# Seven block products for each pair of the last four gate tiles, with the combined inputs formed in the places of q

## The chip, the cores and the metric

One core of a Trainium2 chip runs the whole layer as one program. The metric is the device time of one execution in microseconds (us), the median of several runs. Engines: PE multiplies matrices, DVE, ACT and POOL work on vectors, SP issues transfers; POOL and ACT can issue transfers too. Each engine works through its instructions in the order in which the built program has them, and waits on semaphores for what other engines and transfers deliver.

## The reference

A transformer layer on 1024 tokens of width 1024 with 256 context tokens. The part that matters here is the input projection of the modulated tokens and the gates:

```python
h = x * (1.0 + scale1) + shift1
proj = h @ w_in + b_in                      # q_a, k_a, v_a, q_b, k_b, v_b, then 2 x 1024 gate columns
o_a = _windowed_attention(q_a, k_a, v_a, k_a_c, v_a_c, sink)
o_b = _global_attention(q_b, concat(k_b, k_b_c), concat(v_b, v_b_c))
g_a, g_b = jnp.split(jax.nn.sigmoid(proj[..., OFF_GA:]), 2, axis=-1)
y = (g_a * (o_a @ w_branch_a) + g_b * (o_b @ w_branch_b)) @ w_out
x = _layer_norm(DEEPNORM_ALPHA * x + gate1 * y, ln1_g, ln1_b)
```

A gated convolutional feed-forward part with a second layer norm follows. All inputs and the output are 32-bit floats.

## The kernel before

Every product is made from three matmuls on pairs of a rounded value and its rest: `split` (L335) casts to the high half and subtracts for the low half, `mm3` (L344) adds high x high, high x low and low x high into one PSUM bank of 128x512. `wsplit` (L418) makes such a pair from a 128x512 block of weights: the high half on ACT, the low half on DVE, or on POOL for gate weights.

The stage of the projections holds the modulated x, transposed, as pairs `hT[k]` (hh, hl: 128 rows of the width by 1024 tokens, k from 0 to 7) for its whole length. It runs a list of steps, `order` (L943 on), from the numbers `GORD`: so many gates, then group qa, gates, group qb, gates, group ka (keys and values of tokens 0 to 639), gates, group kb (the other tokens and the context), gates. `GORD = 3, 4, 4, 1, 4` puts one gate between ka and kb and four behind kb. A group step multiplies one k with the group's four or five token tiles (12 or 15 matmuls) and holds a PSUM bank for each of them; a gate (128 of the 2048 gate columns) is two steps of 24 matmuls, one for each half of the tokens (`gate`, L908). It ends with the sigmoid on ACT and a transfer of the result to DRAM (`sgd`). Eight PSUM banks rotate among all of these.

Around the matmuls, a step loads the weights of the step five ahead (`wload1`, three buffers) and splits those of the step three ahead (`wpair`, four pairs of buffers), both in the order of the code. Up to the end of ka the orders of DVE and SP are the code's; behind that a scheduler sets them, and PE's order follows the code of the steps. Between the matmuls `side_step` (L932) takes the work of finished groups from a queue, one piece of each running item at a time. For a key and value tile that is `kv_post` (L628): s1 adds the bias on DVE out of PSUM (L633, tile `kv`, two buffers), turns the first keys (L532 to L540) and splits the values; s2 scales and turns the other keys and makes the pair `ks` (L341, L342); s3 transposes `ks` on PE into `ktr` (L664), four matmuls of 128x128, which ACT copies to the key tables KL and KC. Tiles `pw` (five buffers) hold the intermediate values and `ks`. Sets 0 to 4 are the tiles of ka, 5 to 9 those of kb. Two more sets, `qtr` (L699), transpose q for the first two units of attention.

Before that, q of both branches was written to SBUF tiles `Q[br, t]`, 128x2x512 each, in eight places of a pool (`hslot` names the place of each tile). Attention begins on PE right behind the last gate and reads KL, KC, V and Q in an order that a planner sets.

## Time and profile before

| | |
|---|---|
| median of 3 runs | 1532.02 us (1530.24 to 1532.84) |
| profiled execution | 1530.37 us, span of its instructions 1528.6 us, clock 0.998 |
| PE, DVE, ACT, POOL busy | 1512.9, 1144.8, 802.1, 773.5 us |
| group ka on PE | 220.15 to 247.35 us |
| gate between ka and kb | 247.35 to 258.24 us |
| group kb, with seven sets of transpositions | 258.24 to 288.06 us |
| four gates, with five sets | 288.06 to 333.48 us |

The page of the profile has for each engine its busy time, groups of instructions by line, and 40 slices of the span (the stretch above lies in slices 6 to 9). The views by window, by timeline and by group answer the same for a chosen stretch. A line of the timeline has the start, the duration, engine, line of the code, operation, output and inputs with buffer numbers left out, shape, how many in a row, and in brackets the idle time ahead of it with what ended that. In the groups the mean duration is in ns.

### The profile page before, as it was taken

Reading aid. Unit: us, or ns where it says so; the run is one execution under the profiler, and the core shown is the slowest. Engines: PE = TensorE matmul, PEld = TensorE weight load, DVE = VectorE, ACT = ScalarE, POOL = GpSimd, SP = SyncE. Lnnn points to the kernel's source line nnn. Section 1 sums busy time; section 2 is a strip of 40 time slices with the busy share of each in tenths; the row PEclk is TensorE's granted clock in tenths of the full one; section 3 lists DMA queues with packets and bytes.
Section 4 is the critical chain, followed back from the end, with each engine's and each line's share of the span. In section 5 each row is a group of like instructions: output and inputs, shape, how many; then the busy total and the mean of one; then the engine's idle time right before and its main releaser. Section 6 shows DMA issues by size and latency. Waiting matters only on the chain. (4 is left out here: it accounts for less than half of the span.)

```text
span 1528.6 us, 21924 instructions
## 1 busy us (share of the span) xinstructions
PE 1512.9 (99%) x7652; PEld 1269.9 (83%) x7652; DVE 1144.8 (75%) x1719; ACT 802.1 (52%) x1404; POOL 773.5 (51%) x737
## 2 busy tenths in 40 slices
PE   9999999999999999999999999999999999999997
PEld 7888888888988888888788988888888888888886
DVE  7488847627776777787665878888888887656797
ACT  5422223449887777798332574444444444435543
POOL 0365303418887565574333556666676674021063
PEclk9999999999999999999999999999999999999999
DMA  9667663312256663742460222333334446996723
GB/s 379 236 234 254 213 239 110 100 49 56 57 151 157 176 149 79 169 95 68 169 173 35 97 86 108 112 110 112 112 102 111 110 111 177 373 281 207 253 91 111
DMA packets 111873, 229.73 MB, mean 150 GB/s; under 512 B 13489, under 2 KB 27313, under 8 KB 111666
## 3 DMA queue, kind: packets, MB, share of 16 engines
q1 hardware_dynamic: 96464, 199.20, 39.0%
q0 software_dynamic: 10400, 20.19, 8.4%
q10 hardware_dynamic: 4898, 8.94, 1.6%
q8 instruction: 60, 0.98, 0.3%
q14 instruction: 51, 0.42, 0.1%
HBM read 177.09 MB, written 65.87 MB: 159 GB/s over the span
## 5 line engine op out<-in xcount | busy, mean ns | idle before, releaser
L1151 DVE TENSOR_TENSOR lo<-pt,hi 128x512 fp32r<-128x512 f32 x188 | 126.4, 688 | 42.8 <-ACT hi L1145 41.3
L342 DVE TENSOR_TENSOR ld<-rd,hd 128x1024 fp32r<-128x1024 f32 x77 | 97.8, 1287 | 49.6 <-ACT hd L337 47.4
L1145 ACT CAST hi<-pt 128x512 fp32r<-128x512 f32 x188 | 109.6, 584 | 47.3 <-PE pt L808 39.1
L337 ACT CAST hd<-rd 128x1024 fp32r<-128x1024 f32 x77 | 79.4, 1050 | 85.8 <-PE p L347 55.7
L345 PE MATMUL p<-hd 128*128 128x512 f32 x264 | 103.2, 391 | 0.0
L346 PE MATMUL p<-ld,hd 128*128 128x512 f32 x264 | 102.8, 389 | 0.2 <-DVE ld L342 0.2
L347 PE MATMUL p<-hd,ld 128*128 128x512 f32 x264 | 102.8, 389 | 0.0
L817 PE MATMUL av<-lo,VT 128*128 128x512 f32 x236 | 101.5, 435 | 0.2 <-POOL lo L1151 0.2
L817 PE MATMUL av<-hi,VT 128*128 128x512 f32 x236 | 100.5, 433 | 0.0
L347 PE MATMUL g<-hh,wlg 128*128 128x512 f32 x256 | 99.7, 390 | 0.4 <-POOL wlg L342 0.4
L345 PE MATMUL g<-hh,whg 128*128 128x512 f32 x256 | 99.9, 390 | 0.0
L346 PE MATMUL g<-hl,whg 128*128 128x512 f32 x256 | 99.6, 389 | 0.0
L754 DVE TENSOR_SCALAR_CACHE_REDUCE p<-s,cvt,nmc 128x1024 f32<-128x1024 f32 x64 | 85.8, 1340 | 16.4 <-PE s L721 9.3
L342 POOL TENSOR_TENSOR wlg<-wg,whg 128x512 fp32r<-128x512 f32 x32 | 45.3, 1423 | 99.3 <-ACT whg L337 93.7
L763 ACT ACTIVATE p<-p,nm 128x1024 f32<-128x1024 f32 x64 | 74.0, 1157 | 13.0 <-DVE p L754 12.4
L808 PE MATMUL pt<-ident,p 128*128 128x128 f32 x512 | 76.8, 272 | 0.0
L808 PEld LDWEIGHTS pt<-ident,p 128*128 128x128 f32 x512 | 62.7, 140 | 15.4 <-DVE lo L1151 0.2
L337 ACT CAST wS<-s 128x512 fp32r<-128x512 f32 x76 | 45.3, 620 | 52.1 <-POOL s L1465 51.3
L720 PE MATMUL s<-KL,q 128*128 128x512 f32 (+2 forms) x184 | 72.4, 393 | 0.0
L721 PE MATMUL s<-KL,q 128*128 128x512 f32 (+2 forms) x184 | 69.0, 375 | 0.2 <-DMA q<-q 0.2
L337 ACT CAST wA<-ru 128x512 fp32r<-128x512 f32 x57 | 35.5, 623 | 59.6 <-PE d L347 31.8
L342 DVE TENSOR_TENSOR wS<-s,wS 128x512 fp32r<-128x512 f32 x57 | 55.5, 1000 | 11.1 <-ACT wS L337 11.1
(432 smaller groups left out, 5019.2 us busy)
## 6 DMA issues: line engine op xcount, KB each, us to landing
wml<-in_wmodT_dram SPq DMA_DIRECT2D x48, 512.0 KB
ru<-in_w_up_dram SPq DMA_DIRECT2D x38, 512.0 KB
rd<-td SPq DMA_DIRECT2D x55, 256.0 KB
rd<-sd SPq DMA_DIRECT2D x44, 256.0 KB
rd<-in_w_dn_dram SPq DMA_DIRECT2D x33, 256.0 KB
wm<-in_wmodT_dram SPq DMA_DIRECT2D x16, 512.0 KB
wg<-in_w_g_dram SPq DMA_DIRECT2D x32, 256.0 KB
sgd<-sg ACTq DMA_DIRECT2D x32, 256.0 KB
```

The costliest lines, as they stand in the source:

```text
L337: cast[:] = [nc.scalar.copy(hi, src).ins]
L342: low[:] = [lo_eng.tensor_tensor(out=lo, in0=src, in1=hi.bitcast(F32), op=ALU.subtract).ins]
L345: nc.tensor.matmul(ps, a[0], b[0], start=start, stop=False, skip_group_check=resumed)
L346: nc.tensor.matmul(ps, a[0], b[1], start=False, stop=False, skip_group_check=resumed)
L347: return nc.tensor.matmul(ps, a[1], b[0], start=False, stop=stop, skip_group_check=resumed).ins
L720: nc.tensor.matmul(o, self.q1[:, hs], ks, start=True, stop=False)
L754: nc.vector.tensor_scalar(out=p if self.br else p[:, self.pad + 1:SINK + 1], in0=self.sv[h], scalar1=self.scale()[:, hs] if self.br else - ...
L763: nc.scalar.activation(o, i, AF.Exp, bias=self.nm[:, hs], scale=-1.0, accum_out=acc)
L808: nc.tensor.transpose(tr[:, h * P:(h + 1) * P], src, ident)
L817: nc.tensor.matmul(self.av, v, self.parts[n][low], start=first, stop=self.left == 0)
L1145: nc.scalar.copy(hi, units[u].parts[n])
L1151: e.tensor_tensor(out=lo, in0=src, in1=hi.bitcast(F32), op=ALU.subtract)
```

## The change

The last four gate tiles (12 to 15, two pairs) are computed behind everything else of the stage by a product scheme for 2x2 blocks that takes seven block products in place of eight. For a pair p, the weights are four blocks (row half r of the width, gate tile c), each 512 x 128; the inputs are four blocks as well (half of the width, half of the tokens). Three products, P1, P2 and P4, take weights as they are, four, P6, P5, P7 and P3, take sums and differences of weight blocks, made on POOL (`bsums`). P1, P2 and P3 take x as it is, and P4, P6, P5 and P7 take combined x. Each product is four `mm3`, 12 matmuls. Products share banks where one continues another's sum (P2 on P1, P7 on P6, P3 on P5), and the four outputs of a pair are made from these by copies and sums on ACT and DVE ahead of their sigmoids (`product`).

The combined x needs unrounded, modulated x, and room. So the eight Q tiles are written to DRAM during ka (`away`), x is loaded again into their places (`xload`, during kb and gate 11), modulated on ACT (`xscale`) and combined on DVE (`xsums`, four subtractions for each k and k+4). The pairs of combined x (`tsplit`) go to the second token half of `hT[0..3]`, which gate 11 is the last to read, and to places of x that are done with. The Q tiles come back (`qback`) behind that, into other places than before. The plain weight blocks for the sums (`blocks`) use the buffers of kv_post, and so the queue of side steps is emptied in gate 11, by four more side steps in each of its halves.

`GORD` becomes 3, 4, 4, 0, 1: no gate between ka and kb, and one, gate 11, behind kb, ahead of the fourteen products.

```diff
-GORD = 3, 4, 4, 1, 4
+GORD = 3, 4, 4, 0, 1
+LATE = 12
...
+    SRC = {"P1": (0, 0), "P2": (0, 1), "P4": (1, 1)}
+    SUM = {"P5": (0, 0), "P7": (1, 0), "P6": (1, 1), "P3": (0, 1)}
...
     def wpair(gi, k, a):
+        if gi == "s" and k in SUM:
+            ready[gi, k, a] = wsplit(blk[a, SUM[k]], f"{k}_{a}")
+            return
         wr = ready.pop((gi, k, a, "raw"))
-        if gi == "g":
+        if gi in ("g", "s"):
             ready[gi, k, a] = wsplit(wr, f"g{k}_{a}", "gpsimd")
...
+    plain = len(steps)
+    steps += [("s", n, p) for n in ("P1", "P2", "P4", "P6", "P5", "P7", "P3") for p in (0, 1)]
+
+    def away(br, t):
+        nc.sync.dma_start(qd[br, t], Q[br, t])
...
+    def xload(k):
+        X[k] = onto(hslot["Q%d_%d" % xplace(k)], [P, T], F32, f"xs{k}")
+        nc.sync.dma_start(X[k], xT[k])
+
+    def qback(*moves):
+        places = [hslot["Q%d_%d" % xplace(k)] for _, _, k in moves]
+        for (br, t, _), place in zip(moves, places):
+            home[f"Q{br}_{t}"] = place
+            Q[br, t] = onto(place, [P, 2, HALF], F32, f"Q{br}_{t}")
+            nc.sync.dma_start(Q[br, t], qd[br, t])
...
+    def xscale(k):
+        for n in (k, k + 4):
+            x = X[n]
+            nc.scalar.activation(x, x, AF.Identity, bias=modc[:, n:n + 1], scale=modc[:, 8 + n:9 + n])
+
+    def xsums(k):
+        a, b = k, k + 4
+        for o, p, q in ((xs(a, 1), xs(a, 1), xs(a, 0)), (xs(b, 1), xs(b, 1), xs(a, 1)),
+                        (xs(b, 0), xs(b, 0), xs(b, 1)), (xs(a, 0), xs(b, 1), xs(a, 0))):
+            nc.vector.tensor_tensor(out=o, in0=p, in1=q, op=ALU.subtract)
...
+    def tsplit(n, k):
+        d, hf, m = TP[n]
+        hi = hT[k][m][:, HALF:T]
+        if k not in TL:
+            TL[k] = onto(hslot["Q%d_%d" % xplace(3 + k) if k else "ropet"], [P, T], R32, f"tl{k}")
+        split(xs(d + k, hf), hi, TL[k][:, hsl(m)], nc.scalar, nc.vector if n in ("P4", "P5") else nc.gpsimd)
...
+    def bsums(p):
+        a11, a12, a21, a22 = (blk[p, (r, c)] for r in (0, 1) for c in (0, 1))
+        for o, a, b, op in ((a21, a11, a21, ALU.subtract), (a22, a22, a21, ALU.subtract), (a11, a22, a11, ALU.add),
+                            (a12, a12, a22, ALU.subtract)):
+            nc.gpsimd.tensor_tensor(out=o, in0=a, in1=b, op=op)
...
+    def product(n, p):
...
+        for k in range(4):
+            c = slice(k * P, (k + 1) * P)
+            mm3(ps, (h[:, c], l[:, c]), late_b(n, k), k == 0 and not more, k == 3, more)
...
         if gi == "g":
             gate(k, a)
+            if n >= plain - 2:
+                if a == 0:
+                    xload(3)
+                    xload(7)
+                    xsums(2)
+                else:
+                    xscale(3)
+                    xsums(3)
+                for _ in range(4):
+                    side_step()
...
+        if gi == 0:
+            away(*((1, 2 * k) if k < 4 else (0, (2 * k - 6) % 8)))
+        elif gi == 1:
+            if k in (0, 2, 4):
+                xload(k // 2)
+                xload(k // 2 + 4)
+            if k in (3, 5, 7):
+                xscale((k - 3) // 2)
+            if k in (5, 7):
+                xsums((k - 5) // 2)
```

How instructions stand on PE behind group kb, in the kernel before: `acckb9` is the last matmul of kb, `g12_0` the first half of gate 12, `ktr5` the transpositions of key tile 5. Each half gate is 24 matmuls, of which the first is shown.

```order
L347 MATMUL acckb9_2320<-whkb7_2526,cl7_2560 128x512
L345 MATMUL g12_0_2626<-hh0_210,whg12_0_2554 128x512
...
L345 MATMUL g12_1_2696<-hh0_210,whg12_0_2554 128x512
...
L664 MATMUL ktr5_2750<-identr_59,ks5_2729 128x128 x4
L345 MATMUL g13_0_2783<-hh0_210,whg13_0_2601 128x512
...
L664 MATMUL ktr6_2811<-identr_59,ks6_2764 128x128 x4
L664 MATMUL ktr7_2838<-identr_59,ks7_2825 128x128 x4
L345 MATMUL g13_1_2856<-hh0_210,whg13_0_2601 128x512
...
L664 MATMUL ktr8_2884<-identr_59,ks8_2849 128x128 x4
L664 MATMUL ktr9_2895<-identr_59,ks9_2892 128x128 x4
L345 MATMUL g14_0_2905<-hh0_210,whg14_0_2692 128x512
```

Sets 5 to 9 stand one to two at a time between halves of gates 12, 13 and 14, and gates 14 and 15 follow behind them. The same place in the changed kernel, where `lx0` is the bank of product P1 of the first pair:

```order
L348 MATMUL acckb9_2168<-whkb7_2374,ch7_2445 128x512
L346 MATMUL g11_0_2583<-hh0_218,whg11_0_2440 128x512
...
L670 MATMUL ktr4_2619<-identr_59,ks4_2534 128x128 x4
L670 MATMUL ktr5_2690<-identr_59,ks5_2669 128x128 x4
L670 MATMUL ktr6_2717<-identr_59,ks6_2704 128x128 x4
L670 MATMUL ktr7_2744<-identr_59,ks7_2731 128x128 x4
L346 MATMUL g11_1_2764<-hh0_218,whg11_0_2440 128x512
...
L670 MATMUL ktr8_2798<-identr_59,ks8_2755 128x128 x4
L670 MATMUL ktr9_2809<-identr_59,ks9_2806 128x128 x4
L346 MATMUL lx0_2821<-hh0_218,whgP1_0_2552 128x512
```

Sets 4 to 7 now stand together behind the first half of gate 11, sets 8 and 9 behind its second half, and all products behind these. On DVE in the changed kernel, the last rows ahead of the first two sums of kb (`kv5`, `kv6`; `xs` is x in the places of q):

```order
L343 TENSOR_TENSOR ks4_2534<-kv4_2420,ks4_2534 128x4x64
L1013 TENSOR_TENSOR xs5_2280<-xs5_2280 128x512
L1013 TENSOR_TENSOR xs1_2278<-xs5_2280,xs1_2278 128x512
L1013 TENSOR_TENSOR xs2_2399<-xs2_2399 128x512
L549 TENSOR_TENSOR tbk5_2637<-ropet_148,gcol_149 128x64
L1013 TENSOR_TENSOR xs6_2401<-xs6_2401,xs2_2399 128x512
L554 TENSOR_TENSOR tbk5_2637<-ropet_148,gcol_149 128x2x16 x2
L1013 TENSOR_TENSOR xs6_2401<-xs6_2401 128x512
L1013 TENSOR_TENSOR xs2_2399<-xs6_2401,xs2_2399 128x512
L639 TENSOR_TENSOR kv5_2628<-acckb5_2164,bias_kv_571 128x512
L639 TENSOR_TENSOR kv6_2646<-acckb6_2165,bias_kv_571 128x512
```

Twelve subtractions of x, of which these are the last six, now stand ahead of the sums of kb; four more stand between them and the pairs of key tiles 7 to 9.

More of the change, by code (lines that the diff above doesn't have):

```diff
@@ L380, in layer_kernel @@
     sgd = [dpool.tile([P, T], F32, tag=f"sg{f}", name=f"sgd{f}") for f in range(2 * KT)]
+    qd = {(br, t): dpool.tile([P, 2, HALF], F32, tag=f"qd{br}_{t}", name=f"qd{br}_{t}")
+          for br in (0, 1) for t in range(0, NT, 2)}
     hp = tc.alloc_tile_pool(name="hp", bufs=1, side="left", reuse_waits="tile")
@@ L446, in mod, with hsl @@
                                        accum_out=o)
+    def hsl(hf):
+        return slice(hf * HALF, (hf + 1) * HALF)
     hT = []
@@ L853, in layer_kernel, with gblock @@
     ready = {}
+    SRC = {"P1": (0, 0), "P2": (0, 1), "P4": (1, 1)}
+    SUM = {"P5": (0, 0), "P7": (1, 0), "P6": (1, 1), "P3": (0, 1)}
+    blk = {}
+    def gblock(t, p, r, c):
+        nc.sync.dma_start(t.rearrange("p (a b) -> p a b", b=P), w_g[LATE + 2 * p + r][:, 4 * c:4 * c + 4])
+        return t
     def wload1(gi, k, a):
+        if gi == "s":
+            if k in SRC:
+                ready[gi, k, a, "raw"] = gblock(raw(f"w{k}_{a}"), a, *SRC[k])
+            return
         if gi == "g":
@@ L864, in wpair @@
     def wpair(gi, k, a):
+        if gi == "s" and k in SUM:
+            ready[gi, k, a] = wsplit(blk[a, SUM[k]], f"{k}_{a}")
+            return
         wr = ready.pop((gi, k, a, "raw"))
-        if gi == "g":
+        if gi in ("g", "s"):
             ready[gi, k, a] = wsplit(wr, f"g{k}_{a}", "gpsimd")
@@ L877, in cpair @@
         nc.scalar.activation(cx, cx, AF.Identity, bias=modx[:, k:k + 1], scale=modx[:, 8 + k:9 + k])
-        c = ready["c", k] = [ph1.tile([P, NC], R32, tag="ch", name=f"c{a}{k}", bufs=4) for a in "hl"]
+        t = ph1.tile([P, 2, NC], R32, tag="ch", name=f"ch{k}", bufs=2)
+        c = ready["c", k] = [t[:, 0], t[:, 1]]
         split(cx, *c, nc.vector, nc.vector)
@@ L950, in layer_kernel, with xplace, onto @@
     steps = [(gi, k, a) for gi, k in order for a in ((0, 1) if gi == "g" else (0,))]
+    plain = len(steps)
+    steps += [("s", n, p) for n in ("P1", "P2", "P4", "P6", "P5", "P7", "P3") for p in (0, 1)]
+    def away(br, t):
+        nc.sync.dma_start(qd[br, t], Q[br, t])
+    X = {}
+    def xplace(k):
+        return (0, (14 - 2 * k) % 8) if k > 3 else (1, 2 * k)
+    def onto(place, shape, dt, name):
+        pool, tag = place
+        return pool.tile(shape, dt, tag=tag, name=name, bufs=1)
@@ new lines, in xload, with xs @@
+    def xload(k):
[7 more added lines that the diff above has]
+            nc.sync.dma_start(Q[br, t], qd[br, t])
+    home, TL = {}, {}
+    def xs(k, hf):
+        return X[k][:, hsl(hf)]
@@ new lines, in xscale @@
+    def xscale(k):
[7 more added lines that the diff above has]
+            nc.vector.tensor_tensor(out=o, in0=p, in1=q, op=ALU.subtract)
+    TP = {"P4": (4, 0, 0), "P6": (4, 1, 1), "P5": (0, 1, 0), "P7": (0, 0, 1)}
@@ new lines, in tsplit, with late_b @@
+    def tsplit(n, k):
[4 more added lines that the diff above has]
+        split(xs(d + k, hf), hi, TL[k][:, hsl(m)], nc.scalar, nc.vector if n in ("P4", "P5") else nc.gpsimd)
+    def late_b(n, k):
+        if n in TP:
+            m = TP[n][2]
+            return hT[k][m][:, HALF:T], TL[k][:, hsl(m)]
+        d, hf = {"P1": (0, 0), "P2": (4, 0), "P3": (4, 1)}[n]
+        return [t[:, hsl(hf)] for t in hT[d + k]]
@@ new lines, in blocks @@
+    def blocks():
+        tags = [("pw", PWB)] * 5 + [("kv", KVB)] * 2 + [("bias", 2)]
+        for p in (0, 1):
+            for r, c in ((1, 0), (0, 0), (1, 1), (0, 1)):
+                tag, bufs = tags.pop(0)
+                blk[p, (r, c)] = gblock(ph1.tile([P, 512], F32, tag=tag, name=f"wb{p}_{r}{c}", bufs=bufs), p, r, c)
+    def bsums(p):
[3 more added lines that the diff above has]
+            nc.gpsimd.tensor_tensor(out=o, in0=a, in1=b, op=op)
@@ new lines, in swish, with vsum, sgt @@
+    def swish(f, hf, o, src):
+        sigmoid[:] = [nc.scalar.activation(o, src, AF.Sigmoid, bias=bgc[:, f:f + 1]).ins]
+        nc.scalar.dma_start(sgd[f][:, hsl(hf)], o)
+    def vsum(o, a, b):
+        nc.vector.tensor_tensor(out=o, in0=a, in1=b, op=ALU.add)
+    def sgt(f, hf):
+        return ph1.tile([P, HALF], F32, tag="sg", name=f"sg{f}_{hf}", bufs=2)
+    bank, part = {}, {}
+    def product(n, p):
+        f = LATE + 2 * p
+        key = {"P1": "x", "P2": "x", "P4": "w", "P6": "y", "P7": "y", "P5": "z", "P3": "z"}[n], p
+        more = n in ("P2", "P7", "P3")
+        if not more:
+            bank[key] = acc_tile(f"l{key[0]}{p}")
+        ps = bank[key]
+        h, l = ready.pop(("s", n, p))
+        for k in range(4):
+            c = slice(k * P, (k + 1) * P)
+            mm3(ps, (h[:, c], l[:, c]), late_b(n, k), k == 0 and not more, k == 3, more)
+        if n == "P1":
+            part[p, 1] = ph1.tile([P, HALF], F32, tag="ch", name=f"u1_{p}", bufs=2)
+            nc.scalar.copy(part[p, 1], ps)
+        elif n == "P2":
+            swish(f, 0, sgt(f, 0), ps)
+        elif n == "P6":
+            part[p, 2] = raw(f"u2_{p}")
+            vsum(part[p, 2], ps, part[p, 1])
+        elif n == "P7":
+            u3 = part[p, 1]
+            vsum(u3, ps, u3)
+            o = sgt(f + 1, 1)
+            vsum(o, bank["z", p], u3)
+            vsum(u3, bank["w", p], u3)
+            swish(f + 1, 1, o, o)
+            swish(f + 1, 0, u3, u3)
+        elif n == "P3":
+            u2 = part[p, 2]
+            vsum(u2, ps, u2)
+            swish(f, 1, u2, u2)
@@ L972, in layer_kernel @@
         at(n + 2, cpair, 1)
+        if gi == "s":
+            product(k, a)
+            m = n - plain
+            if m == 0:
+                for q in range(4):
+                    tsplit("P4", q)
+                    tsplit("P6", q)
+                qback((0, 0, 7))
+            elif m == 1:
+                blocks()
+            elif m == 2:
+                bsums(0)
+                bsums(1)
+            elif (k, a) == ("P4", 1):
+                for q in range(4):
+                    tsplit("P5", q)
+            elif (k, a) == ("P6", 1):
+                for q in range(4):
+                    tsplit("P7", q)
+                qback((0, 2, 0), (0, 4, 1), (0, 6, 2), (1, 0, 3))
+            elif (k, a) == ("P7", 1):
+                qback((1, 2, 4), (1, 4, 5), (1, 6, 6))
+                hslot.update(home)
+            continue
         if gi == "g":
             gate(k, a)
+            if n >= plain - 2:
[8 more added lines that the diff above has]
+                    side_step()
+                if a:
+                    assert not queue and not flight
             mods(3 * KT)
@@ L1266, in weight @@
         return h, l
-    def hsl(hf):
-        return slice(hf * HALF, (hf + 1) * HALF)
     def gemm(ps, w, a, n, halves=(0, 1)):
```

## The prediction

> **What bounds the kernel now.** The page's first part comes first, then the table by windows for the stretch that the change touches, then the timelines of PE, DVE and POOL in it. The page says that PE is the bound; the windows (us from the span's start; for each engine busy time and instructions, then clock, DMA share, GB/s) say who is near it there.

> ```profile
> PE 1512.9 (99%) x7652; PEld 1269.9 (83%) x7652; DVE 1144.8 (75%) x1719; ACT 802.1 (52%) x1404; POOL 773.5 (51%) x737
> L345 PE MATMUL g<-hh,whg 128*128 128x512 f32 x256 | 99.9, 390 | 0.0
> 247.35:285.54 38.19, 38.19 (x186) 31.75 (x185) 28.48 (x104) 17.96 (x51) 14.76 (x17) 1.00 0.34 106
> 285.54:307.28 21.74, 21.74 (x104) 18.07 (x103) 18.67 (x54) 8.94 (x28) 13.54 (x16) 1.00 0.24 83
> 307.28:333.48 26.20, 26.20 (x121) 21.69 (x121) 0.00 (x1) 4.93 (x9) 2.59 (x2) 1.00 0.11 41
> ```

> PE is full in all three windows, at clock 1.00. The first runs from the end of group ka to the first sum that DVE takes from group kb: DVE is busy for 28.48 of 38.19 us. The second is DVE's work on the keys of kb: 18.67 of 21.74. In the third DVE does nothing, while PE runs gates for 26.20 us. So PE's gates cover DVE, and the cover is long only because four gates stand last.

> What a gate and a set of transpositions cost on PE, and when the keys are ready:

> ```profile
> 322.80 0.69 ACT L920 ACTIVATE sg<-g,bgc 128x512 f32<-128x512 f32 x1 [4.75 <-PE g L347]
> 328.24 0.69 ACT L920 ACTIVATE sg<-g,bgc 128x512 f32<-128x512 f32 x1 [4.75 <-PE g L347]
> 333.68 0.69 ACT L920 ACTIVATE sg<-g,bgc 128x512 f32<-128x512 f32 x1 [4.76 <-PE g L347]
> 258.00 0.39 PE L347 MATMUL g<-hh,wlg 128*128 128x512 f32 x1
> 258.24 0.46 PE L664 MATMUL ktr<-identr,ks 128*128 128x128 f32 x4
> 258.53 0.46 PE L345 MATMUL acckb<-whkb,hh 128*128 128x512 f32 x1
> 258.83 0.39 PE L346 MATMUL acckb<-wlkb,hh 128*128 128x512 f32 x1
> 287.83 0.39 PE L347 MATMUL acckb<-whkb,cl 128*128 128x512 f32 x1
> 288.06 0.39 PE L345 MATMUL g<-hh,whg 128*128 128x512 f32 x1
> 298.94 0.46 PE L664 MATMUL ktr<-identr,ks 128*128 128x128 f32 x4
> 304.75 0.80 PE L664 MATMUL ktr<-identr,ks 128*128 128x128 f32 x8
> 310.97 0.80 PE L664 MATMUL ktr<-identr,ks 128*128 128x128 f32 x8
> 333.48 0.28 PE L720 MATMUL pt<-KL,q 128*128 128x256 f32 x1
> ```

> Half a gate, 24 matmuls, ends every 5.44 us: 0.227 us for each. The 390 ns of the group are a pipelined matmul's own length and would overstate the saving by 70%. A set of four transpositions delays the rest by about 0.37 us (0.30 to the next matmul, which itself takes 0.07 longer). Group kb ends at 288.06, PE takes the sets of its keys 10.9, 16.7 and 22.9 us later, and attention begins at 333.48.

> **The change part by part.**

> Removed: four gates are 192 matmuls, fourteen products of twelve are 168. 24 x 0.227 = 5.44 us less on PE, all of it on the path since PE has no gap there.

> Moved: the gate between ka and kb goes behind kb, and of the four gates behind kb only this one still lies ahead of the keys' last transpositions. In the orders above, before, set 5 stands after 48 matmuls of gates, sets 6 and 7 after 72, 8 and 9 after 96; now sets 5 to 7 stand after 24 and sets 8 and 9 after 48, all ahead of the first product. PE works in order, so behind each of these sets wait all matmuls that follow. DVE's side:

> ```profile
> 285.54 1.37 DVE L633 TENSOR_TENSOR kv<-acckb,bias_kv 128x512 f32<-128x512 f32 x2 [2.52 <-PE acckb L347]
> 298.79 1.39 DVE L342 TENSOR_TENSOR ks<-kv,ks 128x256 fp32r<-128x256 f32 x1
> 306.86 0.42 DVE L342 TENSOR_TENSOR ks<-kv,ks 128x256 fp32r<-128x256 f32 x1
> 298.58 1.32 POOL L342 TENSOR_TENSOR wlg<-wg,whg 128x512 fp32r<-128x512 f32 x1
> 258.50 0.68 DVE L342 TENSOR_TENSOR wlkb<-wkb,whkb 128x512 fp32r<-128x512 f32 x1
> 259.10 0.28 DVE L532 TENSOR_TENSOR ktp<-kv,ropet 128x128 f32<-128x128 f32 x1
> ```

> From the first sum of kb to the end of key block 7 (ks7) DVE takes 300.18 - 285.54 = 14.6 us, to the last one (ks9) 307.28 - 285.54 = 21.7. With DVE on time, kb would end 10.88 us sooner and one set earlier at 276.8, ks7 would be ready near 289 and ks9 near 296, while PE asks at 282.6 and 288. That already is a wait.

> Added on DVE ahead of it: sixteen subtractions that combine x (L1013), twelve of them ahead of the first sum of kb in DVE's order. A 128x512 subtraction takes 0.60 us from its start to the next one's (258.50 to 259.10): 7.2 us. DVE's 28.48 us of the first window then become 35.7, and the first sum of kb starts at 247.35 + 35.7 = 283.0 at the soonest if DVE has no idle time, against 276.8 if the subtractions fill only idle time: these are the bounds from below. POOL adds to them. The second and fourth row show the same thing at once: ks7's low half, 0.42 us elsewhere, took 1.39 while POOL's subtraction ran from 298.58 to 299.90. Three such low halves of gate weights (1.3 us each) lay in the first window where DVE mostly idled and now meet a dense DVE: up to 3.9 us, so 283.0 to 286.9. I take 284, near the lower end, since not each one meets a DVE operation that it stops.

> [...]

> From the first sum of kb to ks9: the 21.7 us, plus one subtraction of x (three others fit into the 3.07 us in which DVE idled), plus three low halves of combined x (tl) that stand ahead of ks9 in DVE's order, 4 x 0.60 = 2.4, plus two such low halves on POOL, 2.6, less the two low halves of gate weights that no longer fall here (four before, two now), 2.6: 24.1 us. It gives 284 + 24.1 = 308.1; with one set, the first product starts at 308.6. Left without this wait, it would start at 276.8 + 10.88 + 6 x 0.37 = 289.9. PE thus waits 18.7 us in all, most at set 7 and the rest at sets 3 and 9. Set 3 stands inside kb, where DVE is late too.

> Products: 168 x 0.227 = 38.1 us from 308.6. From then on POOL has eleven 1.3 us operations up to and with the low half that the second P4 needs 14 us later, 14.3 us: I take 0.5, from 0 to 2. End 347.2 against 333.48: +13.7.

> Hidden, taken as nothing: eight scalings of x on ACT, nearest row

> ```profile
> L337 ACT CAST hd<-rd 128x1024 fp32r<-128x1024 f32 x77 | 79.4, 1050 | 85.8 <-PE p L347 55.7
> GB/s 379 236 234 254 213 239 110 100 49 56 57 151 157 176 149 79 169 95 68 169 173 35 97 86 108 112 110 112 112 102 111 110 111 177 373 281 207 253 91 111
> 336.62 0.73 ACT L763 ACTIVATE pa<-pa,nm 128x513 f32<-128x513 f32 x1 [0.73 <-POOL pa L1029]
> ```

> 8.4 us, beside ACT's 17.96 of 38.19, and that is their price without this cover. q out, x in and q back are 24 transfers of 0.5 MB, 12.6 MB on SP's queue, with kb's weights and context queued behind; the windows move 41 to 106 GB/s and the first slice of the span showed 379, so some 46 us of spare rate in over 80. A late x stops ACT and the kb casts behind it; weights come five steps ahead, which hides it. The evacuation of products (sums of 0.69 us, sigmoids) lies beside the next product; only the last sum delays ACT, by 0.7 us, which the 0.73 us that the first exponential waits for POOL hide. A transfer of the last gate that keeps an attention tile could cost up to 1.8.

> The profiled execution took 1530.37 us: 1544.1. The median of the runs is 1.65 above it: 1545.7.

> **Rivals.** *DVE fits in.* The twelve subtractions fall into idle time and POOL stops nothing more: first sum 276.8, ks9 21.7 us later and 0.6 for one subtraction that finds no gap, 299.1, first product 299.6, end 337.7: +4.2, 1536.2. For it: 9.7 us of idle in the first window. Against: that window is now 10.9 us shorter.

> *PE does not wait (the other side).* The sets are ready when PE asks, and the whole 5.44 us is gained: 1526.6. It decides from the point where ks7 is done 5.8 us after kb's end, not the 12.1 (300.18 - 288.06) of before; waits of 5.44 us in all make it even. For it: PE shows no wait now. Against: DVE's row above.

> *POOL binds as well.* All three low halves of gate weights stop DVE (286.9); from there all four subtractions count and only one gate operation of POOL drops out (24.1 + 1.8 + 1.3 = 27.2); the block sums hold P4 by 2 us: first product 314.6, end 354.7, +21.2: 1553.2.

> **How the numbers follow.** Forecast 0.62, DVE fits in 0.18, no wait 0.10, POOL binds 0.10. A measurement of this kernel tells about 0.2% (3.1 us) from no change. Slower by more: 0.62 + 0.10 + most of 0.18 = 0.85; within: 0.05, from waits of 2.4 to 8.5 us; faster 0.10. The range goes from 1533, short of the even case, to 1554, past POOL's.

> **What would show it.** Right: PE's waits name DVE ks ahead of transpositions (L670), several us each, between the halves of gate 11 and ahead of the first product; DVE near full from 247 to 308; the first product's start 15 to 25 us after gate 11's. Wrong: no such waits, or waits on DMA (x, q, blocks) or on POOL inside the products; ks7 within 6 us of kb's end; the first sum of kb before 280.

## The result, and the profile after

The changed kernel takes 1551.85 us (median of 4 runs, 1549.80 to 1552.59); the kernel before, run beside it, took 1531.71 us (1530.24 to 1532.84). The ratio is 1.013, with a 95% interval from 1.0112 to 1.0147: slower. The span of the profiled execution is 1549.9 us against 1528.6, so 21.3 us are to be found.

The page, busy time of the engines and PE's two rows of slices (tenths of each fortieth of the span; PEclk is the granted clock):

```profile
PE 1514.9 (98%) x7628; PEld 1269.4 (82%) x7628; DVE 1187.5 (77%) x1761; ACT 825.6 (53%) x1436; POOL 800.0 (52%) x751
PE   9999999599999999999999999999999999999997
PEclk9999999799999999999999999999999999999999
```

Twenty-four matmuls fewer, yet 2 us more of busy PE: in slice 8, from 271 to 310, PE idles and its clock falls. The waits of PE over the whole run (sum, times, longest) say for whom; the kernel before has neither of these two rows:

```profile
PE ktr L670 <- DVE ks L343: 17.8, 5, 3.9
PE sx L727 <- DMA q<-q: 1.9, 1, 1.9
```

PE's timeline shows the five waits, what follows the last one, and the start of attention (start, duration, in brackets the idle time before and its releaser):

```profile
275.12 0.51 PE L670 MATMUL ktr<-identr,ks 128*128 128x128 f32 x4 [2.96 <-DVE ks L343]
290.31 0.72 PE L670 MATMUL ktr<-identr,ks 128*128 128x128 f32 x4 [3.47 <-DVE ks L343]
294.77 0.75 PE L670 MATMUL ktr<-identr,ks 128*128 128x128 f32 x4 [3.75 <-DVE ks L343]
299.19 0.75 PE L670 MATMUL ktr<-identr,ks 128*128 128x128 f32 x4 [3.67 <-DVE ks L343]
311.60 0.72 PE L670 MATMUL ktr<-identr,ks 128*128 128x128 f32 x4 [3.95 <-DVE ks L343]
312.12 0.76 PE L346 MATMUL lx<-hh,whgP 128*128 128x512 f32 x1
312.67 0.63 PE L347 MATMUL lx<-hl,whgP 128*128 128x512 f32 x1
313.10 0.63 PE L348 MATMUL lx<-hh,wlgP 128*128 128x512 f32 x1
317.63 0.40 PE L347 MATMUL lx<-hl,whgP 128*128 128x512 f32 x1
352.99 0.28 PE L726 MATMUL pt<-KL,q 128*128 128x256 f32 x1
```

These are sets 3, 5, 6, 7 and 9. Attention starts at 352.99 in place of 333.48, 19.5 us later. After set 9 the first matmuls start 0.43 us apart (312.67 to 313.10), not 0.227, until 317.4. The windows of that stretch (busy time of PE, PEld, DVE, ACT, POOL, then the granted clock, DMA share, GB/s) show the same at three places:

```profile
270.00:280.00 10.00, 7.04 (x30) 5.47 (x29) 10.00 (x21) 5.32 (x14) 5.06 (x5) 0.83 0.57 180
300.00:307.20 7.20, 7.20 (x25) 5.64 (x25) 4.96 (x8) 5.75 (x15) 5.38 (x5) 0.74 0.11 36
312.00:317.40 5.40, 5.40 (x16) 4.24 (x16) 0.06 (x1) 1.28 (x3) 3.76 (x3) 0.50 0.73 248
317.40:353.00 35.60, 35.60 (x158) 29.26 (x157) 17.38 (x21) 16.37 (x27) 18.58 (x14) 1.00 0.39 128
```

By the starts of the matmuls, the last fifteen of kb take 1.6 us more than at full pitch, the second half of gate 11 takes 2.0 more (7.46 in place of 5.44) and the 48 matmuls of P1 and P2 take 2.5 more. The ledger up to attention: -5.44 for the matmuls left out, +17.8 of waits, +6.1 of slow clock make 18.5 of the 19.5; four of the sets that waited are themselves slower (0.7 in place of 0.45 us), which is about the rest. Behind the start of attention 1.8 us more are lost.

DVE on the way to the last keys: the first sum of kb, and the stretch from ks8 to ks9:

```profile
282.21 1.27 DVE L639 TENSOR_TENSOR kv<-acckb,bias_kv 128x512 f32<-128x512 f32 x2
300.83 0.42 DVE L343 TENSOR_TENSOR ks<-kv,ks 128x256 fp32r<-128x256 f32 x1
302.63 0.85 DVE L343 TENSOR_TENSOR tl<-xs,hh 128x512 fp32r<-128x512 f32 x1 [0.22 <-ACT hh L338]
304.02 0.68 DVE L343 TENSOR_TENSOR tl<-xs,hh 128x512 fp32r<-128x512 f32 x1
305.29 1.38 DVE L565 TENSOR_TENSOR kv<-kv,ssk 128x128 f32<-128x128 f32 x1 [0.59 <-POOL ssk L561]
307.85 0.93 DVE L343 TENSOR_TENSOR tl<-xs,hh 128x512 fp32r<-128x512 f32 x1 [1.19 <-POOL tl L343]
308.70 1.35 DVE L342 CAST ks<-kv 128x256 fp32r<-128x256 f32 x1
310.09 1.36 DVE L343 TENSOR_TENSOR ks<-kv,ks 128x256 fp32r<-128x256 f32 x1
```

The last key block's low half, 0.42 us for ks8, takes 1.36, its cast 1.35 and its scaling 1.38, while POOL splits combined x and weights (305.23 to 311.2 without a gap). Three splits of x (tl), which only the products need, stand between. The end of the same stretch in the kernel before:

```profile
303.58 0.43 DVE L342 TENSOR_TENSOR ks<-kv,ks 128x256 fp32r<-128x256 f32 x1
305.46 1.36 DVE L341 CAST ks<-kv 128x256 fp32r<-128x256 f32 x1 [0.57 <-POOL kv L655]
306.86 0.42 DVE L342 TENSOR_TENSOR ks<-kv,ks 128x256 fp32r<-128x256 f32 x1
```

From the end of ks8 to the end of ks9 are 3.3 us before (304.01 to 307.28) and 10.2 us in the change (301.25 to 311.45). From the first sum of kb to ks8 the two hardly differ, 18.5 and 19.0 us.

### The profile page after: what moved, and what is told of

Same layout as the page of the kernel before. It is cut to its first block, busy times and chain, and to the rows that moved or that the text cites. A ratio compares the mean times of both kernels' runs of the same rounds, so it can differ in the third digit from the quotient of the medians.

```text
span 1549.9 us, 22042 instructions
## 1 busy us (share of the span) xinstructions
PE 1514.9 (98%) x7628; PEld 1269.4 (82%) x7628; DVE 1187.5 (77%) x1761; ACT 825.6 (53%) x1436; POOL 800.0 (52%) x751
## 3 DMA queue, kind: packets, MB, share of 16 engines
q10 hardware_dynamic: 4898, 8.94, 1.5%
## 4 chain that ended last, share of the span: by engine, by line
PE 88%; DVE 6%; DMA 2%; POOL 2%; issue 1%; ACT 1%; SPq 0%; DVEq 0%; POOLq 0%; ACTq 0%
PE av L823 7%; PE pt L814 6%; PE p L347 3%; PE p L348 3%; PE p L346 3%; PE g L348 3%; PE s L726 3%; PE g L347 3%; PE g L346 3%; PE s L727 3%; PE c L346 2%; PE c L348 2%; PE a L346 2%; PE d L346 2%; PE a L348 2%; PE d L348 2%
## 5 line engine op out<-in xcount | busy, mean ns | idle before, releaser
L338 ACT CAST hd<-rd 128x1024 fp32r<-128x1024 f32 x77 | 79.5, 1050 | 86.0 <-PE p L348 54.9
L346 PE MATMUL p<-hd 128*128 128x512 f32 x264 | 103.3, 391 | 0.0
L347 PE MATMUL p<-ld,hd 128*128 128x512 f32 x264 | 102.8, 389 | 0.1
L348 PE MATMUL g<-hh,wlg 128*128 128x512 f32 x192 | 75.5, 393 | 0.4 <-POOL wlg L343 0.4
L346 PE MATMUL g<-hh,whg 128*128 128x512 f32 x192 | 75.7, 394 | 0.0
L347 PE MATMUL g<-hl,whg 128*128 128x512 f32 x192 | 75.4, 393 | 0.0
L1333 POOL TENSOR_TENSOR lo<-ptr,hi 128x512 fp32r<-128x512 f32 x48 | 62.7, 1305 | 2.0
```

Of the source, the lines that this page charges most:

```text
L338: cast[:] = [nc.scalar.copy(hi, src).ins]
L346: nc.tensor.matmul(ps, a[0], b[0], start=start, stop=False, skip_group_check=resumed)
L347: nc.tensor.matmul(ps, a[0], b[1], start=False, stop=False, skip_group_check=resumed)
L348: return nc.tensor.matmul(ps, a[1], b[0], start=False, stop=stop, skip_group_check=resumed).ins
L1333: e.tensor_tensor(out=lo, in0=src, in1=hi.bitcast(F32), op=ALU.subtract)
```

## The experiments

Times are medians; the ratio is to runs of the kernel before on the same chip, with its 95% interval. "Attention" is the first matmul of attention in the profile (before: 333.48; the change: 352.99).

| run | time us | ratio | attention |
|---|---|---|---|
| e1_cover | 1543.11 | 1.0070 (1.0053 to 1.0087) | 345.00 |
| e2_no_xsums | 1547.0 (one run) | | 347.39 |
| e3_filled | 1560.79 (one run) | | 361.10 |
| e4_splits | 1553.56 (one run) | | 355.42 |
| e5_lows | 1541.5 | 1.0064 (1.0049 to 1.0079) | 343.94 |
| e6_onegate | 1538.16 | 1.0044 (1.0032 to 1.0056) | 339.14 |
| e7_sumslater | 1543.87 | 1.0076 (1.0061 to 1.0092) | 345.99 |
| e8_beforegate | 1533.74 | 1.0011 (1.0002 to 1.0021) | 334.48 |
| e9_sumslast | 1530.57 | 0.9995 (0.9986 to 1.0004) | 330.92 |
| e10_dvesplits | 1532.25 | 1.0000 (0.9990 to 1.0009) | 331.81 |
| e11_behind4 | 1531.22 | 0.9997 (0.9988 to 1.0006) | 332.21 |
| e12_behind4 | 1531.64 | 1.0001 (0.9993 to 1.0010) | 333.64 |

### Cover given back: e1_cover

```diff
-GORD = 3, 4, 4, 0, 1
+GORD = 3, 4, 2, 0, 3
```

> Two of the four gates ahead of ka go behind kb (order of gates 3, 4, 2, 0, 3 in place of 3, 4, 4, 0, 1), so that the last key sets stand after 24, 48, 72 and 96 gate matmuls again, as in the kernel before. Theory (PE waits because the gates that covered DVE and POOL are gone): the waits of PE for ks behind kb fall from 14.8 us (sets 5, 6, 7 and 9) to under 1 us, the one of about 3 us inside kb may stay, the granted clock is 1.00 behind kb, and the time is the kernel before's less 5.4 us for the 24 matmuls, up to less 2.4: 1526 to 1530 us. Rival (DVE has too much work in any order): the waits move into ka or kb and sum to 8 us or more, 1535 to 1545. Rival (the products and the transfers of q cost by themselves): no waits for ks, but 1545 or more.

The waits behind kb are gone, as the theory said, and the one inside kb stayed (3.63 us). But the time is 1543.1: of the 20 us that the change costs only 8.7 came back. PE now waits elsewhere, on POOL, inside the products; first PE's row, then POOL's rows ahead of it:

```profile
309.73 0.80 PE L348 MATMUL lx<-hh,wlgP 128*128 128x512 f32 x1 [7.15 <-POOL wlgP L343]
```

```profile
302.07 5.17 POOL L1042 TENSOR_TENSOR wb<-wb,wb 128x512 f32<-128x512 f32 x4 [2.32 <-DMA wb<-in_w_g_dram]
307.20 1.26 POOL L343 TENSOR_TENSOR tl<-xs,hl 128x512 fp32r<-128x512 f32 x1
308.42 1.26 POOL L343 TENSOR_TENSOR wlgP<-wP,whgP 128x512 fp32r<-128x512 f32 x1
```

The low half of P2's weights stands behind the block sums (L1042), which themselves waited 2.3 us for their blocks. The late keys had hidden this. In the changed kernel POOL was in time, with 2.8 us to spare at the second P4: its low half ended at 326.03, PE asked at 328.78.

### Less work on DVE: e2_no_xsums

```diff
             if k in (5, 7):
-                xsums((k - 5) // 2)
+                pass
```

> Leaves out the first eight subtractions that combine x (those of pairs 0 and 1 that stand ahead of the first sum of kb), so the last four gate tiles are not the reference's. Theory (DVE's amount of work sets the keys' time): the first sum of kb comes 3 to 5 us sooner than 282.2 (limited by the end of kb on PE, about 278 without the wait at set 3), ks9 about as much sooner, span 1545 to 1547 against 1549.9. Rival (POOL's stops and the slow clock set it, not the amount): first sum within 1 us of 282.2 and span above 1548.5.

The span is 1545.2 us, 4.7 us less. DVE's first sum of kb and the low half of ks9:

```profile
279.83 1.27 DVE L639 TENSOR_TENSOR kv<-acckb,bias_kv 128x512 f32<-128x512 f32 x2
304.75 1.37 DVE L343 TENSOR_TENSOR ks<-kv,ks 128x256 fp32r<-128x256 f32 x1
```

The sum comes 2.4 us sooner, a little less than the 3 to 5 expected, and ks9 5.3. So the amount of work counts, but it is not the whole: PE still waits 10.2 us for keys behind kb, and 2.3 us inside kb for POOL's split of q in place of set 3. Even this low half takes 1.37 us.

### PE kept busy: e3_filled

```diff
+FILLERS = {3: 11, 5: 13, 6: 14, 7: 14, 9: 15}
...
+            if t in FILLERS:
+                for _ in range(FILLERS[t]):
+                    nc.tensor.matmul(tr.rearrange("p h q -> p (h q)").bitcast(F32), identr, hT[0][0][:, 0:HALF],
+                                     start=True, stop=True)
             for h in range(4):
                 nc.tensor.transpose(tr[:, h], ks[:, h], identr)
```

> 67 matmuls of 128x512 whose result nothing reads stand ahead of key sets 3, 5, 6, 7 and 9 (11, 13, 14, 14 and 15 of them, 0.227 us each), so that PE works while it waits. Theory (a wait of 3 to 4 us is followed by about 4 us at a lower granted clock): clock 1.00 from 270 to 320, the second half of gate 11 takes 5.4 us in place of 7.5, DVE still sets when the sets come (set 7 near 299), the first product starts at 309 to 312 and its matmuls have a pitch of 0.227 at once: span 1545 to 1548. Rival (the pitch of 0.43 us comes from something else than idling): the pitch stays and the span is 1549 or more.

On the clock it decides; windows of the second half of gate 11 and of the first products:

```profile
302.00:307.70 5.70, 5.70 (x29) 4.69 (x27) 2.62 (x8) 5.35 (x14) 1.22 (x3) 1.00 0.50 128
311.80:320.00 8.20, 8.20 (x40) 6.72 (x38) 3.90 (x3) 1.98 (x4) 8.12 (x7) 1.00 0.20 66
```

Both run at 1.00 where they had 0.74 and 0.50, with the same matmuls. One wait that was left (3.96 us, ahead of set 5) is followed by 0.77 in the window from 287 to 302. So the idling takes the clock. The time went the other way, since the fillers ahead of set 9 held PE until 311.6, when ks9 had been ready at 305.5, and the scheduler gave POOL another order: the products waited for POOL's low halves for 1.6 and 4.3 us.

### The splits of combined x behind the keys: e4_splits

```diff
-                for q in range(4):
-                    tsplit("P4", q)
-                    tsplit("P6", q)
+                with tc.issue_after(KLAST["dve"]), tc.issue_after(KLAST["pool"]):
+                    for q in range(4):
+                        tsplit("P4", q)
+                        tsplit("P6", q)
```

KLAST holds the last instruction of key block 9 on each of the two engines; what stands in the block follows it there.

> The splits of the combined x for P4 and P6 (tl: four low halves on DVE, four on POOL) are issued behind the last key block's low half on DVE and behind its product with the gain on POOL. Theory (the seven low halves tl that stand ahead of ks9 cost it twice, by their own time and by POOL stopping DVE, more than the 4.4 us allowed): ks9 is done at 304.5 to 307.5 in place of 311.4, the first product starts near 307.7 when gate 11 ends, the slow clock behind it goes too: span 1542 to 1545. Rival (DVE's chain of one key block is the limit): ks9 stays within 1 us and the span within 1.5 us of 1549.9. Rival (the splits are needed too soon): P4 waits for tl by 2 us or more.

DVE's end of ks9, PE's first product, and what came of it:

```profile
306.22 1.41 DVE L343 TENSOR_TENSOR ks<-kv,ks 128x256 fp32r<-128x256 f32 x1
```

```profile
308.78 0.46 PE L346 MATMUL lx<-hh,whgP 128*128 128x512 f32 x1
329.33 0.80 PE L348 MATMUL lw<-hh,wlgP 128*128 128x512 f32 x1 [5.46 <-POOL wlgP L343]
```

ks9 is done at 307.6 in place of 311.4, PE does not wait for it, and the first product starts at 308.78, 3.3 us sooner and at full pitch (0.30 and then 0.23 us). That part held. All of it and 2.4 us more went back at P4: POOL had five block sums (320.73 to 327.6) ahead of the low half of its weights.

### POOL relieved: e5_lows, e6_onegate, e7_sumslater

```diff
-            ready[gi, k, a] = wsplit(wr, f"g{k}_{a}", "gpsimd")
+            ready[gi, k, a] = wsplit(wr, f"g{k}_{a}", "vector" if k in ("P2", "P4") else "gpsimd")
```

> As e1_cover, and the low halves of the weights of P2 and P4 are taken on DVE in place of POOL, where they stood behind eight block sums of 1.3 us. Theory (with the keys on time POOL is the next bound, 7.15 + 0.38 us of waits and the slow clock behind them): no wait of the products of over 0.5 us, the 48 matmuls of P1 and P2 at a pitch of 0.23 us, time 7.5 to 10 us under e1_cover's 1543.1: 1533 to 1536. Rival (DVE is late with them, since they stand behind the splits of x): the waits go over to DVE, 1 us or more. Rival (the order of POOL was not the cause): the wait stays.

The wait went over to DVE (6.07 us for the same low half), as the rival said, and the time, 1541.5 us, missed the 1533 to 1536. Why the splits of x ahead of it are late shows in the next run, which differs in one line:

```diff
-GORD = 3, 4, 2, 0, 3
+GORD = 3, 4, 1, 1, 3
```

> As e5_lows, with the gates as 3, 4, 1, 1, 3: one gate stands between ka and kb again, as before the change, three stand behind kb. Theory (the wait of 3.6 us inside kb and the slow clock after it come from the cover that this gate gave): no wait inside kb, nor for ks, nor in the products; the time is the kernel before's less 5.4 us, up to less 2.4: 1526 to 1530 us. Rival (all sixteen subtractions now stand ahead of the first sum of kb on DVE): waits for ks behind kb of 2 us or more; or waits in ka, where only one gate is left ahead: 1531 to 1537.

With one gate between ka and kb the wait inside kb fell from 3.6 to 1.4 us and no slow clock follows it (behind it a matmul takes 0.39 us, as elsewhere at full pitch); waits for ks behind kb: none. P2 still waits 4.66 us, and the time, 1538.16 us, is past the rival's range too. DVE's and then POOL's rows ahead of it:

```profile
290.18 1.27 DVE L343 TENSOR_TENSOR tl<-xs,hh 128x512 fp32r<-128x512 f32 x1 [11.82 <-ACT hh L338]
301.91 0.69 DVE L343 TENSOR_TENSOR tl<-xs,hh 128x512 fp32r<-128x512 f32 x1 [10.46 <-POOL tl L343]
302.52 1.75 DVE L343 TENSOR_TENSOR wlgP<-wP,whgP 128x512 fp32r<-128x512 f32 x1
```

```profile
295.42 5.24 POOL L1042 TENSOR_TENSOR wb<-wb,wb 128x512 f32<-128x512 f32 x4 [1.33 <-DMA wb<-in_w_g_dram]
300.62 4.79 POOL L343 TENSOR_TENSOR tl<-xs,hl 128x512 fp32r<-128x512 f32 x3
```

DVE has nothing to do for 10.46 us and waits for POOL's first split of x. The second tl lies in the place of the x that this split still reads (`xplace(3 + k)` for k = 1 is where x tile 4 stood), POOL takes block sums first, and P2's low half stands behind the second tl on DVE.

> As e5_lows, with the first eight subtractions of x written behind the first gate halves after kb in place of inside kb (DVE's order then has at most two of them ahead of ks3). Theory (the wait at set 3 inside kb comes from the subtractions ahead of it): it falls from 3.6 to under 1.5 us, and the time lies 2 to 5 us under e5_lows. Rival (it comes from the gate that no longer stands between ka and kb): it stays over 2.5 us and the time is e5_lows's within 1.5 us.

In e7_sumslater the call of `xsums` for pairs 0 and 1 moves from kb to the first two gate halves behind it. The wait of set 3 went (0; the split of q then takes 0.6), so in this order of gates their place does make it late; e11_behind4 below shows that they are not its only cause. But they come back behind kb, where set 7 waits:

```profile
279.44 0.72 PE L670 MATMUL ktr<-identr,ks 128*128 128x128 f32 x4 [3.66 <-DVE ks L343]
```

The time is 2.4 us above e5_lows's, not below it: the wait went as the theory said, but its sum was wrong, since DVE has no room behind kb either.

### The gate alone: e8_beforegate

```diff
-GORD = 3, 4, 4, 1, 4
+GORD = 3, 4, 4, 0, 5
```

> The kernel before, with the one gate between ka and kb moved to the end: gates 3, 4, 4, 0, 5; no products, no combined x, no transfers of q. Theory (the subtractions are what makes set 3 late, and five gates cover the last sets): PE does not wait and the time is that of before within 2 us. Rival (the gate between ka and kb is the cover that set 3 needs): a wait of 2 us or more inside kb and 2 to 5 us more time: 1534 to 1537.

No wait for any key, one of 1.26 us for the context's cast inside kb, 2 us more time (ratio 1.0011), between the theory and its rival. Moving the gate without the products is nearly free as long as five gates follow.

### The chain cut: e9_sumslast, e10_dvesplits

```diff
+                turned = low[0]
                 qback((0, 0, 7))
...
-                bsums(0)
-                bsums(1)
+                with tc.issue_after(turned):
+                    bsums(0)
+                    bsums(1)
```

> As e6_onegate, and POOL takes the eight block sums behind the four low halves of combined x (tl for P6). Theory (the 4.7 us wait of P2 in e6_onegate is a chain: DVE's low half of P2's weights stands behind its second tl, which writes over the x that POOL's first tl still reads, and that one stands behind the block sums): POOL's first tl ends near 292 in place of 302, the wait of P2 falls under 0.5 us, the 48 matmuls of P1 and P2 have a pitch of 0.23 us, and the time is 6 to 8 us under e6_onegate's profiled 1535.6: 1527.5 to 1530, a gain of 0.1 to 0.3% over before. Rival (the block sums are then late): P6 waits for its weights by 2 us or more. Rival (the products cost more than 168 matmuls by themselves): no wait, but 1533 or more.

POOL takes the splits first; DVE's low half of P2 follows at once; PE runs from the first product to attention without a wait:

```profile
288.65 1.30 POOL L343 TENSOR_TENSOR tl<-xs,hl 128x512 fp32r<-128x512 f32 x1 [5.62 <-ACT hl L338]
296.69 12.74 POOL L1042 TENSOR_TENSOR wb<-wb,wb 128x512 f32<-128x512 f32 x8
```

```profile
292.62 0.39 PE L346 MATMUL lx<-hh,whgP 128*128 128x512 f32 x1
```

The fourteen products take 38.3 us (292.62 to 330.92, 168 x 0.228). Attention starts 2.56 us before the kernel before's: -5.44, and +2.7 for waits that are left (1.43 and 0.27 for keys inside kb, 1.03 for POOL at a gate between qa and qb). The median is 1530.57 us, just past the range that was expected and no difference from before that can be told. The profiled span is that of before, too (1528.6 us): behind attention this run loses about what it had won. From the first matmul into `b`, the product that follows attention, to the first into `y` it takes 42.3 us, against 39.5 before, and its granted clock is 0.50 for 6.83 us there. The last section shows the rows.

> As e6_onegate, with the low halves tl for P6 on DVE in place of POOL, so that no instruction of DVE waits for POOL's block sums. Theory (the same chain, cut at another place): no wait of P2 over 0.5 us, time as e9_sumslast within 2 us, 1527.5 to 1531. Rival (POOL's block sums stop DVE's twelve low halves, 1.3 us or more each in place of 0.69, as rows of the kernel before and of the changed kernel show): P2 or P4 waits for DVE by 1 to 4 us, 1531 to 1536.

The other cut (`tsplit` of P6 with DVE's subtraction) does the same: no wait in the products, attention at 331.81, ratio 1.0000. The wait of 1 us or more at P2 or P4 that its rival named did not come.

### What is left: e11_behind4, e12_behind4

```diff
-                xsums((k - 5) // 2)
+                with tc.issue_after(LAST[0]):
+                    xsums((k - 5) // 2)
```

LAST[0] is the low half of ks4 on DVE.

> As e9_sumslast, with the first eight subtractions of x issued on DVE behind the low half of ks4, the last key block of ka. Theory (the 1.4 us wait at set 3 and the 0.3 us at set 1 in e9_sumslast come from the three subtractions that stand ahead of ks1 to ks3): both go, attention starts near 329.3 in place of 330.9, 4.2 us before the kernel before's 333.5, and the time is 1526 to 1529.5 us, a ratio of 0.996 to 0.999. Rival (all sixteen subtractions now stand between ks4 and the first sum of kb): the keys of kb are late, waits for ks behind kb of 1 us or more, attention at 331 or later.

The theory fell: with no subtraction ahead of ks0 to ks3, set 3 waits longer than in e9_sumslast (1.98 us, not 1.43), and there is a new wait of 0.67 us for the context's cast. So the subtractions are not what keeps set 3 late here. Its row on PE:

```profile
240.18 0.52 PE L672 MATMUL ktr<-identr,ks 128*128 128x128 f32 x4 [1.98 <-DVE ktp L544]
```

Attention starts at 332.21, as late as the rival said, but without the waits for keys behind kb that the rival gave as its reason.

> As e11_behind4, with the gates as 3, 3, 2, 1, 3: one gate goes from between qa and qb to between qb and ka. Theory (the 1.0 us for which a gate between qa and qb waits for POOL's low half in e9_sumslast comes from where that gate's weights fall beside POOL's work on q): the wait changes with the place, and the start of attention and the time follow it: 1 us sooner without it, up to 1.5 later if new waits show. No rival predicts more than 2 us either way: 1525 to 1531.

The gate's wait went from 1.14 to 0.85 us, and the time is the same. The profile is of the longest of this kernel's twelve runs, 1535.85 us with a median of 1531.64, so the start of its attention, 333.64, is not typical of it. No version beats the kernel before by more than the measurement tells.

## Why the prediction was right, and where it was off

The verdict, the mechanism and its place were right: the change takes away the cover under which DVE made the keys, PE waits for key sets, and the end comes later by more than the matmuls left out. The forecast of 1545.7 us was 6.15 us short. By its own steps:

- **Removed, 5.44 us.** Right: the products take 38.3 us without waits in e9_sumslast, forecast 38.1.
- **First sum of kb at 284.** It came at 282.2, DVE dense as argued (busy for 33.87 of the 34.86 us from 247.35), 0.8 us sooner than the 283.0 that the step called the soonest for a full DVE. The other bound, 276.8, is where PE ends kb; in the kernel before the first sum came 2.5 us ahead of that end. e2_no_xsums shows the subtractions as part of the term, 2.4 us for eight.
- **From the first sum to ks9, 24.1 us.** This is the term that was mis-sized: 29.2 us (282.21 to 311.4), so the first product started at 312.12, not 308.6. It would have been later still without the luck that the first sum came 1.8 us sooner than forecast. Against the kernel before, the stretch grew by 7.5 us, and 6.9 of these lie between ks8 and ks9. The step counted two splits of x and two low halves of weights on POOL; the trace has three of each in the stretch (splits at 301.65, 306.48 and 308.20, weights at 284.65, 305.23 and 309.87), 2.6 us more at the step's own price of 1.3. And it priced the splits of x at their own length. While POOL worked without a gap, three DVE instructions of ks9 took 3.1 us more than their undisturbed 0.3 to 0.42 us; the cast among them took 1.36 us in the kernel before as well, so 2.0 of the 3.1 are new. DVE also stood for 1.19 us for POOL's split. e4_splits moves the splits behind ks9 on both engines and gets 3.3 of the 3.5 us back; the shares of the two engines were not measured apart.
- **DVE beside POOL.** The forecast had one row for it, 1.39 us beside 0.42. The trace has more like it: the low half and the scaling of ks9, with two inputs, took 1.36 and 1.38 us, and the cast, with one, took 1.35, against 0.42, 0.29 and 0.28 for the same three of set 7 (298.71, 298.50 and 297.84). That POOL's work held them is the author's estimate from the POOL rows beside them (305.23 to 311.2 without a gap); no run tried it alone. The forecast took too few such meetings.
- **PE waits 18.7 us, most at set 7.** 17.8 us, but in five shares of 3.0 to 4.0 us. Five waits are not one lump of that size: the clock fell three times with them (the next point); what it does with one lump was not run.
- **Products, 38.1 + 0.5.** 40.9 us: the 0.5 for POOL did not fall due, and a term was missing, the clock after the waits. The prediction had PE at 0.227 us a matmul wherever it works. Here 2.5 us of slow clock (in the products' first 48 matmuls) lie behind the last wait and thus on the path. Of the 3.6 us of it ahead of set 9, some was hidden, since set 9 waited for DVE anyway; how much wasn't separated.
- **Transfers taken as hidden.** Right up to attention: PE waits for no transfer of q, x or the blocks. Behind its start 1.8 us more go, about as much as one wait for a turned q takes there (1.9 us, the second row of PE's waits above). Whether the change causes it isn't shown: from the start of attention to the end of the span are 1195.1 us before, 1196.9 in the change, and 1194.7 (e6_onegate) to 1196.3 (e4_splits) in the other runs with products whose clock stays at 1.00 there. The rest, 1197.1 (e8_beforegate, without products) to 1200.4 (e12_behind4), have 3.4 to 10.2 us at a clock of 0.50 there.

Added up: 3.5 for ks9, 2.3 in the products, 1.8 behind them are the 7.6 us between the forecast's 13.7 and the measured 21.3 of the span. The forecast of the median added 1.65 us to that of the profiled run, which is why its error is 6.15.

Of the rivals, *PE does not wait* and *DVE fits in* fell. *POOL binds as well* came near in size (1553.2 us), but only one of its three parts came: its 27.2 us from the first sum to ks9 are nearer to the 29.2 than the forecast's 24.1. The first sum did not come at its 286.9, and POOL did not hold P4, where it was ready 2.8 us ahead. It is the next bound, though, as e1_cover and e4_splits show, the latter giving back all that it won.

Left open: what keeps set 3 late in e11_behind4, and whether the 1.9 us wait for q behind the start of attention belongs to the change.

## What to carry to other kernels

Where matmuls also serve as cover for another engine, price a saving of matmuls by that engine's chain: ask when its last result is ready and how many matmuls stand ahead of its use. When one wait is taken away, look at once for the engine that was only just in time behind it; here keys, POOL's low halves and a reused place came one after the other, and of a saving of 5.44 us nothing that could be measured was left even with all three mended. A split that two engines share in turn should stand behind the work that is waited for, not where the scheduler finds a gap, and ahead of what is needed later than it: e4_splits did the first alone and lost it again at P4, and with the block sums behind the splits (e9_sumslast) no product waited. A difference of 1 to 3 us between two single profiled runs can also be the clock: 2.8 us between e9_sumslast and the kernel before, as the next section shows.

## What the runs showed of the hardware

```profile
241.05 0.51 PE L672 MATMUL ktr<-identr,ks 128*128 128x128 f32 x4 [2.07 <-DVE ktp L544]
```

The stretches, two of e11_behind4 and two of e12_behind4 (PE's busy time is the number behind the length, the clock the third from the end):

```profile
236.60:240.01 3.41, 1.60 (x8) 0.98 (x6) 3.09 (x12) 3.13 (x8) 1.52 (x3) 1.00 0.21 67
240.01:243.42 3.41, 3.24 (x19) 2.85 (x20) 3.41 (x12) 1.53 (x6) 0.00 (x0) 1.00 0.73 221
238.54:241.95 3.41, 1.34 (x11) 0.94 (x11) 3.41 (x16) 2.06 (x3) 0.53 (x1) 1.00 0.07 18
241.95:245.37 3.42, 3.42 (x9) 2.67 (x9) 3.42 (x8) 2.25 (x7) 0.00 (x0) 0.50 0.98 275
```

Counted this way in the kernel before and in the change, from the first record of the clock to the last stretch that has matmuls behind it, the three stretches at 1.00 ahead of the three falls of the clock in the change have 2.08, 3.27 and 2.94 us of idle PE; every other one at 1.00 has 1.67 us (the kernel before, 732.86 to 736.28) or less, and 1.00 followed.

The same waits cost nothing beyond their length in one run, and 2.8 us more in another (42.3 us in place of 39.5, see e9_sumslast). Behind attention PE waits 1.67 and 1.00 us for weights both in the kernel before and in e9_sumslast. In the kernel before, the end of a stretch at 736.28 lies between the two waits: 1.67 us of idle, and the clock stays at 1.00. In e9_sumslast the end of a stretch at 734.63 lies inside the second wait, so that the stretch ahead of it has 1.90 us of idle, and the clock is 0.50 for the next 6.83 us. The first row is of the kernel before, the others of e9_sumslast:

```profile
732.86:736.28 3.42, 1.75 (x8) 1.04 (x6) 1.11 (x2) 2.05 (x4) 1.15 (x2) 1.00 0.51 182
731.22:734.63 3.41, 1.51 (x6) 0.57 (x4) 1.21 (x2) 2.48 (x3) 1.65 (x3) 1.00 0.51 143
734.63:741.46 6.83, 6.06 (x14) 4.79 (x15) 2.39 (x2) 0.00 (x0) 4.04 (x4) 0.50 0.48 167
```
